# Four chains of four heads, or one chain of sixteen with its operands in DRAM: the RWKV-7 stage of a hybrid trunk

## The chip, the cores and the metric

The kernel runs on one core of a Trainium2 chip. The metric is the device time of one execution in microseconds. Five engines work beside each other: PE (TensorE, matrix products), DVE (VectorE), ACT (ScalarE), POOL (GpSimd) and SP (SyncE, which here issues nearly all DMAs). Each takes its instructions strictly in its own order and waits at an instruction until what it needs is there.

## The reference

One layer of a decoder trunk on x of 1 x 1024 x 1024, all float32: a normalised input goes through one projection to 7424 columns and from there into three branches (causal pooling, RWKV-7 time mixing, cross attention into 256 memory tokens), which are gated, merged and projected; a ConvFFN follows. The change touches the RWKV-7 branch: 16 heads of 64 values, each with a 64 x 64 state that runs through 1024 steps.

```python
def rwkv7_scan(r, w, k, v, kk_neg, kk_a):
    ...
    def step(state, inp):
        rt, wt, kt, vt, an, bn = inp
        sa = jnp.einsum('bhvk,bhk->bhv', state, an)
        state = state * wt[:, :, None, :] + sa[..., None] * bn[:, :, None, :] + vt[..., None] * kt[:, :, None, :]
        yt = jnp.einsum('bhvk,bhk->bhv', state, rt)
        return state, yt
...
    y = rwkv7_scan(rh, wh, kh, vh, -kk, kk * ah)
    mu = jnp.mean(y, axis=-1, keepdims=True)
    var = jnp.mean(jnp.square(y - mu), axis=-1, keepdims=True)
    y = ((y - mu) * lax.rsqrt(var + LNX_EPS)).reshape(B, S, RWKV_WIDTH)
    y = y * ln_x_w.astype(f32) + ln_x_b.astype(f32)
    bonus = jnp.sum(rh * kh * r_k.astype(f32), axis=-1, keepdims=True) * vh
    y = y + bonus.reshape(B, S, RWKV_WIDTH)
    return y.astype(dt) * g
```

## The kernel before

Everything lies with channels on the partitions and time along the row. The big projections keep float32 precision by splitting both operands into a high and a low part: mm3 (L165 to L171) issues three matmuls of 128x128 by 128x512, hh with whi, hl with whi and hh with wlo. These are the **wide** matmuls. in_block (L304) is one column block of the input projection: eight k by two halves of the time, 16 calls of mm3, 48 wides. Its weights come as four tiles wraw of 128 KB through SP, and ACT (L126) and POOL (L132) make whi and wlo of them.

The time of 1024 is cut into 16 chunks of 64 (C, NCH). Inside a chunk the recurrence is turned into products and a triangular system; from chunk to chunk a state is carried. The sixteen heads are eight pairs (two heads fill 128 partitions). rwkv_group (L455) handles two pairs, and it runs four times, g = 0 to 3. One group does, in this order:

- **Preparation**: decay and learning rate from two small products (psu), square sums of k for its norm (square_sums, L441, products phd), a scan and two exponentials, the r blocks by in_block, and on DVE and ACT the tiles AR, BK, then products ps1 and ps2 (L572, L579) of which masked parts go to NT, RB and AR, bonus (L530, to DRAM as d_bv), the scaling of BK, and its transposes pt to BKN (L595). HV holds the values, turned by the products pv.
- **Solve**: a triangular inverse of 32x32 blocks on DVE alone, a chain of 31 steps of two instructions each (L615, L617), with transposes at both ends (L609, L618, L619). Meanwhile fill_to(95 * g + 95) gives PE wide blocks to do that belong to the pool, query and gate columns and are needed by nothing here (L620; filled is the log, 16 entries to a block, so six blocks to a group). Then the result is copied into NT (L623), and products pz and pw (L631, L639) join the blocks.
- **Chain** (L653 to L716): 16 chunks, in each three **visits** of PE to small products of 64x64: pr (what the state gives the right-hand side), then py and pu (the system applied), then ph and py (the state and the output). After pr, DVE copies it to Rs; after pu, DVE and ACT copy its halves to HV; after ph, DVE adds the decayed state Hd; ACT makes the next Hd and copies py into AR.
- **Output norm** (L722 to L738): per pair, a square, a product pvar that sums it over a head, the root, three DVE steps with d_bv and d_g read from DRAM (gt), and d_y written.
- **group_kv** (L432): the k and v blocks of the next group, four in_blocks, evacuated by ACT and DVE (shifted, L309).

A scheduler lays the instructions of each engine out from a model of their durations; the code's order, the waits and hints by later (L206, an order without a semaphore) bind it. Where PE would wait, the scheduler puts in wides from blocks that stand later in the code. A chain chunk of one group has 20 small products; the wides between its visits come from the fill blocks and from group_kv. PSUM is eight banks: psg for wides (two tags by two), pss two, psk and psc one each. After the four groups the memory attention begins (products pmm, L787), with the eight fill blocks that are left.

Of the kernel before, what the change touches and what calls it, by code (L numbers as in the profile page):

```python
# [17 lines left out]
P = 128  # L18
T = 1024
# [25 lines left out]
def trunk_kernel(ctx: ExitStack, tc: tile.TileContext, xT, memT, pvec, w_in, w_kv, w_upd, w_upg,  # L45
# [19 lines left out]
    d_bv = dtile([8, P, T], "d_bv")  # L65
    d_y = dtile([8, P, T], "d_y")
# [237 lines left out]
    def in_block(j, evac, c=0, log=None):  # L304
        ws = load_w(w_in[j], KC, c=c)
        for t0, _ in HALVES:
            evac(t0, gemm(ws, hrhs(t0), log=log))
# [34 lines left out]
    ld = lr.tile([P, T], FR, name="ld")  # L342
    la = lr.tile([P, T], FR, name="la")
# [97 lines left out]
    def square_sums(src, scale, sq):  # L441

        sp = rw.tile([P, 2, 2, 512], FR, name="sp", tag="NT")
        for n, (t0, _) in enumerate(HALVES):
            s = slice(t0, t0 + 512)
            for d in (sp[:, n, 0], sq[:, s]):
                later(A.activation(d, src[:, s], AF.Square, scale=scale), late[0])
            V.tensor_tensor(sp[:, n, 1], sq[:, s], sp[:, n, 0].bitcast(F32), op=ALU.subtract)
        for n, (t0, _) in enumerate(HALVES):
            ps = pss.tile([P, 512], F32, name="phd", tag="s")  # L450
            PE.matmul(ps, bonesr, sp[:, n, 0], start=True, stop=False)
            PE.matmul(ps, bonesr, sp[:, n, 1], start=False, stop=True)
            yield slice(t0, t0 + 512), ps

    def rwkv_group(g, kv):  # L455
        tagA, tagB, tagC = ([f"X{i}{(g + n) % 3}" for i in range(2)] for n in range(3))
        AR = rw.tile([P, 2, 3, T], F32, name="AR", tag="AR")
        Dc = rw.tile([P, 2, NCH], F32, name="Dc", tag="Dc")
# [20 lines left out]
        table(LN_EXP)  # L479
        vs = []  # L480
# [9 lines left out]
        for i in range(2):  # L490
# [7 lines left out]
            for s, ps in square_sums(t0_, col("k_k", p), t5_):  # L498
                rstd(t5_[:, s], ps, 1)
# [7 lines left out]
            V.tensor_copy(Dc[:, i], c3(t3_)[:, :, C - 1])  # L507
# [37 lines left out]
        HV = rw.tile([P, 2, NCH, 2, C], F32, name="HV", tag="HV")  # L545
        for i in range(2):
            for c0 in (0, 8):
# [5 lines left out]
                A.copy(HV[64:128, i, c0:c0 + 8, 0], ps[64:128])  # L553
                A.copy(HV[0:64, i, c0:c0 + 8, 1], ps[0:64])

# [6 lines left out]
        for i in range(2):  # L562
            us = slice(NCH * i, NCH * i + NCH)
            for c0 in range(0, NCH, 4):
# [17 lines left out]
                V.tensor_tensor(c3(AR[lo, i, 2])[:, cs], ps[lo, :, 1], bc(mstrict, lo), op=ALU.mult)  # L582
            for b in range(2 if i == 0 else 0):
# [3 lines left out]
            for c in range(n):  # L587
                A.activation(BK[i][:, c], BK[i][:, c], AF.Identity, scale=Dc[:, i, c:c + 1])
            if n < NCH:
                V.tensor_tensor(BK[i][:, n:], BK[i][:, n:],  # L590
                                Dc[:, i, n:].unsqueeze(2).broadcast_to([P, NCH - n, P]), op=ALU.mult)
            for c0 in range(0, NCH, 4):
# [3 lines left out]
                A.copy(BKN[i][:, c0:c0 + 4], ps)  # L596

# [11 lines left out]
        V.transpose(X, S.rearrange("p u t -> p t u"))  # L609
# [10 lines left out]
        fill_to(95 * g + 95)  # L620
# [23 lines left out]
        for i in range(2):  # L644
            for e in range(2):
                V.tensor_tensor(RB[i][:, e], RB[i][:, e], mincl.unsqueeze(1).broadcast_to([P, NCH, C]),
                                op=ALU.mult)


        lo, up = slice(0, 64), slice(64, 128)  # L650
        Hn = rw.tile([P, 2, C], F32, name="Hn", tag="Hn")
        Hd = rw.tile([P, 2, C], F32, name="Hd", tag="Hd")
        turn = [0]  # L653

        def bank(name):
            turn[0] ^= 1
            return (psc if turn[0] else psk).tile([P, 2, C], F32, name=name, tag="c" if turn[0] else "k")

        def visit(products, after):

            for (out_, l, r), kw in products:
                m = PE.matmul(out_, l, r, **kw)  # L662
                if after is not None:
# [4 lines left out]
        ready = None  # L668
        for c in range(NCH):
            t = slice(c * C, (c + 1) * C)  # L670
            once = dict(start=True, stop=True)
            pr = bank("pr")
            py = pss.tile([P, 2, C], F32, name="py", tag="s")
# [6 lines left out]
            Rs = rw.tile([P, 2, C], F32, name="Rs", tag="Rs", bufs=1)  # L680
# [3 lines left out]
            for i in range(2 if c else 0):  # L684
                kw = dict(start=i == 0, stop=False)
                row.append(((py[lo, i], HV[lo, i, c, 0], AR[lo, i, 1, t]), kw))
                row.append(((py[up, i], HV[up, i, c, 1], AR[up, i, 1, t]), kw))
            row += [((pu[q, i], NT[q, i, c], Rs[q, i]), once) for i in range(2) for q in (lo, up)]
            visit(row, made if c else None)
            V.tensor_copy(HV[lo, :, c, 0], pu[lo])  # L690
            ready = A.copy(HV[up, :, c, 1], pu[up]).ins
            row = []
            if c + 1 < NCH:
                ph = bank("ph")
                for i in range(2):
                    row.append(((ph[up, i], BKN[i][:, c, 64:128], HV[:, i, c, 1]), once))
                    row.append(((ph[lo, i], BKN[i][:, c, 0:64], HV[:, i, c, 0]), once))
            for i in range(2):
                kw = dict(start=c == 0 and i == 0, stop=i == 1)
                row.append(((py[lo, i], HV[:, i, c, 0], RB[i][:, 0, c]), kw))  # L700
                row.append(((py[up, i], HV[:, i, c, 1], RB[i][:, 1, c]), kw))
            visit(row, ready)
            if c + 1 < NCH:
                for q, e in ((lo, 0), (up, 1)):
                    if c == 0:
                        ready = V.tensor_copy(HV[q, :, 1, e], ph[q]).ins
                    else:
                        ready = V.tensor_tensor(HV[q, :, c + 1, e], ph[q], Hd[q], op=ALU.add).ins  # L708
                if c + 2 < NCH:
# [4 lines left out]
                    for i in range(2):  # L714
# [5 lines left out]
        for i in range(2):  # L720
            p = 2 * g + i
            y = AR[:, i, 1]  # L722
            gt = rw.tile([P, 2, T], F32, name="gt", tag=tagA[i])
            SP.dma_start(gt[:, 0], d_bv[p])
            SP.dma_start(gt[:, 1], d_g[p])
            yq = rw.tile([P, T], F32, name="yq", tag=tagC[i])
            for t0, _ in HALVES:
                s = slice(t0, t0 + 512)
                sq = yq[:, s]
                A.activation(sq, y[:, s], AF.Square)  # L730
                ps = pss.tile([P, 512], F32, name="pvar", tag="s")
                PE.matmul(ps, bones, sq, start=True, stop=True)
                rstd(sq, ps, 2, 1.0 / 64)
                V.tensor_tensor(y[:, s], y[:, s], sq, op=ALU.mult)
# [974 lines left out]
```

## Time and profile before

| | us |
|---|---|
| runs | 2018.13, 2022.89, 2023.48 |
| median | 2022.89 |
| profiled execution | 2021.79 |
| its span | 2020.1 |
| RWKV stage, from the first psu to pmm | 95.2 to 972.0 |

The profile is one execution. Its page gives busy times by engine and by slices of the span; the timeline gives each instruction's start and length; the view of lines groups instructions by line, tile and shape with the mean of one; the view of waits says for which instruction of which engine an engine stood still. A tile on the left of an arrow is written, those on the right are read. One small product of the program shows up as two passes in the trace (x8 is four products), since a float32 product runs in two; a wide matmul is one. Lines of the profile are those of the code printed above.

### The profile page before, as it was taken

The page shows a single profiled execution, that of the slowest core. Times are in us where ns is not written, and L with a number is a line of the kernel's source. Part 1 is how long each engine was busy: PE and PEld are TensorE (multiplying, and loading weights), DVE is VectorE, ACT ScalarE, POOL GpSimd, SP SyncE. Part 2 cuts the span into 40 slices and gives each one's busy share as a digit, 9 for nine tenths or more (in the row PEclk, how much of TensorE's full clock was granted, in tenths as well). Part 3 has the DMA queues.
Part 4 walks back from the last instruction along what each step waited for, and adds up shares of the span by engine and source line. Part 5 has one row for each costly group of instructions (what it writes and reads, how often), then busy time and mean ns, then how long its engine had stood idle before and what let it go on. Part 6 is the DMA issues. An engine that isn't in the chain of part 4 may idle for free.

```text
span 2020.1 us, 34003 instructions
## 1 busy us (share of the span) xinstructions
PE 1977.1 (98%) x12218; PEld 1556.0 (77%) x12218; DVE 1374.0 (68%) x2227; ACT 1065.6 (53%) x2254; POOL 779.6 (39%) x867
## 2 busy tenths in 40 slices
PE   8999999999999999999999999999999999999997
PEld 6777767776778667776878888887878888888886
DVE  8577437664668347743696553658889888878698
ACT  6684348623773358434566334546554454545544
POOL 4411113121222122110232355555579988832441
PEclk9999999999999999999999999999999999999999
DMA  4312111120222121222525544545332222279776
GB/s 155 128 34 84 62 64 58 66 84 23 89 64 84 33 92 40 83 68 80 196 97 168 175 136 126 182 146 177 99 97 87 89 79 84 92 219 236 163 186 147
DMA packets 175689, 220.77 MB, mean 109 GB/s; under 512 B 16544, under 2 KB 127264, under 8 KB 175520
## 3 DMA queue, kind: packets, MB, share of 16 engines
q1 hardware_dynamic: 162592, 203.39, 31.1%
q0 software_dynamic: 11856, 14.16, 4.4%
q8 instruction: 96, 1.57, 0.3%
q10 hardware_dynamic: 1072, 1.05, 0.2%
q14 instruction: 73, 0.60, 0.1%
HBM read 169.25 MB, written 49.28 MB: 108 GB/s over the span
## 4 chain that ended last, share of the span: by engine, by line
PE 47%; DVE 2%; DMA 2%; issue 1%; ACT 0%; SPq 0%; POOL 0%; ACTq 0%; DVEq 0%; POOLq 0%
PE psg L168 7%; PE psg L170 7%; PE psg L169 7%; PE psf L169 5%; PE psf L170 5%; PE psf L168 5%; PE psd L169 3%; PE psd L170 3%; PE psd L168 3%; DMA Q<-in_w_fdn 1%; PE ptr L900 0%; DVE ts L842 0%; PE psn L1175 0%; PE po L168 0%; PE psco L170 0%
## 5 line engine op out<-in xcount | busy, mean ns | idle before, releaser
L132 POOL TENSOR_TENSOR wlo<-wraw,whi 128x256 fp32r<-128x256 f32 x464 | 393.8, 859 | 953.7 <-ACT whi L126 775.0
L168 PE MATMUL psg<-hh,whi 128*128 128x512 f32 x928 | 379.7, 409 | 11.4 <-ACT whi L126 5.9
L170 PE MATMUL psg<-hh,wlo 128*128 128x512 f32 x928 | 377.8, 407 | 0.4
L169 PE MATMUL psg<-hl,whi 128*128 128x512 f32 x928 | 377.4, 407 | 0.5 <-DVE hl L254 0.5
L126 ACT CAST whi<-wraw 128x256 fp32r<-128x256 f32 x472 | 182.2, 403 | 223.3 <-PE psg L169 109.1
L168 PEld LDWEIGHTS psg<-hh,whi 128*128 128x128 f32 x928 | 175.6, 189 | 51.2 <-ACT whi L126 5.9
L170 PEld LDWEIGHTS psg<-hh,wlo 128*128 128x128 f32 x928 | 175.4, 189 | 42.7 <-POOL wlo L132 5.8
L169 PEld LDWEIGHTS psg<-hl,whi 128*128 128x128 f32 x928 | 175.5, 189 | 39.8 <-issue 1.9
L1035 POOL TENSOR_TENSOR wt<-a,wt 128x256 fp32r<-128x256 f32 x136 | 156.6, 1175 | 35.9 <-ACT wt L1034 35.8
L169 PE MATMUL psd<-f,u 128*128 128x512 f32 x292 | 113.9, 390 | 0.2 <-DVE f L1451 0.2
L170 PE MATMUL psd<-f,u 128*128 128x512 f32 x292 | 113.8, 390 | 0.0
L168 PE MATMUL psd<-f,u 128*128 128x512 f32 x292 | 113.3, 391 | 0.2 <-ACT f L1447 0.2
L170 PE MATMUL psf<-h2h,wt 128*128 128x512 f32 x272 | 106.1, 390 | 0.9 <-POOL wt L1035 0.9
L168 PE MATMUL psf<-h2h,wt 128*128 128x512 f32 x272 | 106.0, 390 | 0.0
L169 PE MATMUL psf<-h2l,wt 128*128 128x512 f32 x272 | 106.0, 390 | 0.0
L1049 DVE SCALAR_TENSOR_TENSOR d<-z,pv,d 128x1023 f32<-128x1023 f32 x68 | 100.4, 1479 | 2.3
L708 DVE TENSOR_TENSOR HV<-ph,Hd 64x128 f32<-64x128 f32 x112 | 32.3, 289 | 72.7 <-PE ph L662 45.5
L1035 POOL TENSOR_TENSOR wt<-s,wt 128x256 fp32r<-128x256 f32 x68 | 79.6, 1189 | 3.5 <-ACT wt L1034 2.8
L169 PE MATMUL psf<-t,wt 128*128 128x512 f32 x204 | 79.5, 390 | 0.0
L170 PE MATMUL psf<-t,wt 128*128 128x512 f32 x204 | 79.5, 390 | 0.0
L168 PE MATMUL psf<-t,wt 128*128 128x512 f32 x204 | 79.5, 390 | 0.0
L1047 ACT ACTIVATE d<-z,pv 128x1024 f32<-128x1024 f32 x34 | 42.4, 1246 | 66.4 <-DVE z L1129 50.7
(429 smaller groups left out, 4708.2 us busy)
## 6 DMA issues: line engine op xcount, KB each, us to landing
wraw<-in_w_in SPq DMA_DIRECT2D x232, 128.0 KB, 2.4
a<-in_w_fup SPq DMA_DIRECT2D x128, 128.0 KB, 2.4
d_zg<-st SPq DMA_DIRECT2D x48, 256.0 KB, 2.7
wraw<-in_w_fup SPq DMA_DIRECT2D x80, 128.0 KB, 2.5
fraw<-d_f SPq DMA_DIRECT2D x33, 256.0 KB, 4.5
wraw<-in_w_prwkv SPq DMA_DIRECT2D x64, 128.0 KB, 2.5
wraw<-in_w_o SPq DMA_DIRECT2D x64, 128.0 KB, 2.6
d_f<-d SPq DMA_DIRECT2D x16, 512.0 KB, 3.4
```

What stands on the lines that cost most here:

```text
L126: i = A.copy(hi, src)
L132: (V if lo_on_dve[0] else G).tensor_tensor(lo, src, hi.bitcast(F32), op=ALU.subtract)
L168: first = PE.matmul(ps, wh, xh, start=start, stop=False)
L169: PE.matmul(ps, wh, xl, start=False, stop=False)
L170: last_mm[0] = PE.matmul(ps, wl, xh, start=False, stop=stop).ins
L708: ready = V.tensor_tensor(HV[q, :, c + 1, e], ph[q], Hd[q], op=ALU.add).ins
L1035: low = eng.tensor_tensor(w[1][:, us], src[u], w[0][:, us].bitcast(F32), op=ALU.subtract)
L1047: A.activation(d, z, AF.Identity, scale=col("cw2", j), bias=col("cb", j))
L1049: V.scalar_tensor_tensor(d[:, n:], z[:, :T - n], col(cw, j), d[:, n:], op0=ALU.mult, op1=ALU.add)
```

## The change

The four groups keep only the preparation and the solve. What the chain needs of them is written to DRAM (d_ar, d_rb, d_bk, d_nt, d_hv, laid out by pairs of chunks), and one function, chain, then runs the 16 chunks once for all eight pairs. A visit has four times the products, and each state tile (pr, pu, ph, Rs, Hn, Hd) is 128x512 instead of 128x128; copies out of PSUM are four times as wide and a quarter in number. The operands of two chunks come back by load(b), double-buffered.

The square sums of both pairs are made at the start of a group (lengths). The product of RB with mincl moves from after the solve to before the spill. group_kv of the next group moves from after the chain to before the solve, and the tags of the big tiles rotate by two instead of one. The fill blocks are dealt anew: up to entry 32, 48, 64 and 160 in the four solves (2, 1, 1 and 6 blocks), then inside the chain up to entry 172 + 148 * v // 47 ahead of visit v, and up to 384, all 24 blocks, after it. The output norm runs for two chunks at a time inside the chain (outputs), on all eight pairs. PSUM banks, the number of small products and the number of wides are the same.

```diff
+    d_ar = dtile([NCH // 2, P, 4, 2, 3, 2 * C], "d_ar")
+    d_rb = dtile([NCH // 2, P, 4, 2, 2, 2 * C], "d_rb")
+    d_bk = dtile([NCH // 2, P, 4, 2, 2, P], "d_bk")
+    d_nt = dtile([NCH // 2, P, 4, 2, 2 * C], "d_nt")
+    d_hv = dtile([NCH // 2, P, 4, 2, 2 * C], "d_hv")
...
     def group_kv(g, kv):
...
-            t = rw.tile([P, 2, T], F32, name=f"kv{i}", tag=f"X{i}{g % 3}")
+            t = rw.tile([P, 2, T], F32, name=f"kv{i}", tag=f"X{i}{2 * g % 3}")
...
     def rwkv_group(g, kv):
...
+        def lengths():
+            for i in range(2):
+                for s, ps in square_sums(kv[i][:, 0], col("k_k", 2 * g + i), tHV[:, i, 1], sp[:, i]):
+                    rstd(tHV[:, i, 1, s], ps, 1)
+
         if g:
+            lengths()
             table(SIGMOID)
...
+            for e in range(2):
+                V.tensor_tensor(RB[i][:, e], RB[i][:, e], mincl.unsqueeze(1).broadcast_to([P, NCH, C]),
+                                op=ALU.mult)
+                spill(d_rb, (g, i, e), RB[i][:, e])
+            for e in range(3):
+                SP.dma_start(d_ar[:, :, g, i, e].rearrange("c p t -> p c t"),
+                             AR[:, i, e].rearrange("p (c t) -> p c t", t=2 * C))
...
+        nxt = group_kv(g + 1, []) if g < 3 else None
         tb1 = rw.tile([P, 2, 32, 32], F32, name="tb1", tag=tagB[1])
...
-        fill_to(95 * g + 95)
+        if g == 3:
+            fill_to(96)
+        fill_to((32, 48, 64, 160)[g], solve if g == 3 else None)
...
+    def outputs(b, y, q):
+        bt = slice(b * 2 * C, (b + 1) * 2 * C)
+        gt = []
+        for src, e in ((d_bv, "ld"), (d_g, "la")):
+            gt.append(lr.tile([P, 8, 2 * C], F32, name="gt", tag=e))
+            SP.dma_start(gt[-1], src[:, :, bt].rearrange("n p t -> p n t"))
...
+        for n in (0, 4):
+            ns = slice(n, n + 4)
+            y_, q_ = y[:, ns], q.rearrange("p (n t) -> p n t", t=2 * C)
+            A.activation(q_, y_, AF.Square)
+            ps = pss.tile([P, 512], F32, name="pvar", tag="s")
+            PE.matmul(ps, bones, q, start=True, stop=True)
+            rstd(q, ps, 2, 1.0 / 64)
+            V.tensor_tensor(y_, y_, q_, op=ALU.mult)
...
+    def chain(fills):
...
+        def load(b):
+            ar, nt = ring[:, b % 2], pair[:, b % 2, 0]
+            hv = rw.tile([P, 8, 2, 2, C], F32, name="hv", tag=f"X{b % 2}2")
+            rb = rw.tile([P, 8, 2, 2 * C], F32, name="rb", tag=f"X{b % 2}1")
+            bk = rw.tile([P, 8, 2, P], F32, name="bk", tag=f"X{b % 2}0")
+            for q, e in ((up, 0), (lo, 1)):
+                SP.dma_start(hv[q, :, :, e], d_hv[b, q].rearrange("p g i (u s) -> p (g i) u s", u=2))
+            SP.dma_start(ar, d_ar[b].rearrange("p g i e t -> p (g i) e t"))
+            SP.dma_start(nt, d_nt[b].rearrange("p g i t -> p (g i) t"))
+            SP.dma_start(bk, d_bk[b].rearrange("p g i u s -> p (g i) u s"))
+            SP.dma_start(rb, d_rb[b].rearrange("p g i e t -> p (g i) e t"))
...
         def visit(products, after):
-            for (out_, l, r), kw in products:
+            wide = fill_to(fills(visits[0]))
+            visits[0] += 1
+            for n, ((out_, l, r), kw) in enumerate(products):
                 m = PE.matmul(out_, l, r, **kw)
+                if n == 0:
+                    later(m, wide)
...
+        load(0)
+        load(1)
         for c in range(NCH):
+            b, u = divmod(c, 2)
+            if u == 0 and 0 < b < NCH // 2 - 1:
+                load(b + 1)
...
-            for i in range(2):
-                row.append(((pr[up, i], AR[ko, i, 2, t], HV[ko, i, c, 1]), once))
-                row.append(((pr[lo, i], AR[ke, i, 0, t], HV[ke, i, c, 0]), once))
+            for i in range(8):
+                row.append(((pr[up, i], ar[ko, i, 2, t], hv[ko, i, u, 1]), once))
+                row.append(((pr[lo, i], ar[ke, i, 0, t], hv[ke, i, u, 0]), once))
...
-            A.copy(AR[:, :, 1, t], py)
+            A.copy(y[:, :, t], py)
+            if u:
+                outputs(b, y, root)
...
     for g in range(4):
         kv = rwkv_group(g, kv)
+    chain(lambda v: 172 + 148 * v // 47)
+    fill_to(384)
```

How the instructions stand shows in the order of each engine. PE before, one chunk in the chain of a group (psg is a wide, the others small products; x4 is four in a row):

```order
L662 MATMUL pr<-HV,AR 64x64 x4
L170 MATMUL psg<-hh,wlo 128x512
L662 MATMUL py<-AR,HV 64x64 x4
L662 MATMUL pu<-Rs,NT 64x64 x4
L168 MATMUL psg<-hh,whi 128x512
L169 MATMUL psg<-hl,whi 128x512
L170 MATMUL psg<-hh,wlo 128x512
L168 MATMUL psg<-hh,whi 128x512
L662 MATMUL ph<-HV,BKN_7881 64x64 x2
L662 MATMUL ph<-HV,BKN_7882 64x64 x2
L662 MATMUL py<-RB_7879,HV 64x64 x2
L662 MATMUL py<-RB_7880,HV 64x64 x2
```

PE after, one chunk in the single chain (hv, ring, pair, bk and rb are the tiles loaded from DRAM, in the places of HV, AR, NT, BKN and RB):

```order
L738 MATMUL pr<-hv,ring 64x64 x16
L173 MATMUL psg<-hh,whi 128x512
L738 MATMUL py<-ring,hv 64x64 x16
L738 MATMUL pu<-Rs,pair 64x64 x16
L174 MATMUL psg<-hl,whi 128x512
L175 MATMUL psg<-hh,wlo 128x512
L173 MATMUL psg<-hh,whi 128x512
L174 MATMUL psg<-hl,whi 128x512
L175 MATMUL psg<-hh,wlo 128x512
L173 MATMUL psg<-hh,whi 128x512
L174 MATMUL psg<-hl,whi 128x512
L738 MATMUL ph<-hv,bk 64x64 x16
```

Each stretch of small products is four times as long, and there is one such chunk where there were four. In other chunks a gap between visits holds up to some forty wides.

DVE before, where the solve of the second group begins (tb are its tiles; from L615 the 31 steps follow, without a break):

```order
L590 TENSOR_TENSOR BK_3130<-BK_3130,Dc 128x1024
L604 COPY tb_3615<-NT 32x512 x2
L646 TENSOR_TENSOR RB_3492<-RB_3492,mincl 128x1024
L609 STREAM_TRANSPOSE tb_3615<-tb_3615 128x1024
L610 MEMSET tb_3615 128x1024
L611 MEMSET tb_3615 128x32
L615 TENSOR_TENSOR tb_3721<-tb_3615 128x31
L617 TENSOR_TENSOR tb_3615<-tb_3615,tb_3721 128x31
```

DVE after, the same place (kv are the k and v of the next group, sp its square sums):

```order
L598 TENSOR_TENSOR RB_2621<-RB_2621,mincl 128x1024
L611 TENSOR_TENSOR BK_2258<-BK_2258,Dc 128x1024
L627 COPY tb_2752<-NT 32x512 x2
L324 SCALAR_TENSOR_TENSOR kv_2866<-zc,pv,kv_2866 128x1
L326 SCALAR_TENSOR_TENSOR kv_2866<-psg,pv,kv_2866 128x511
L633 STREAM_TRANSPOSE tb_2752<-tb_2752 128x1024
L454 TENSOR_TENSOR sp<-tHV,sp 128x512
L634 MEMSET tb_2752 128x1024
L322 COPY zc<-psg 128x1
L326 SCALAR_TENSOR_TENSOR kv_2866<-psg,pv,kv_2866 128x511
L635 MEMSET tb_2752 128x32
```

The evacuations of the next group's k and v and the subtractions of its square sums now stand among the steps of the solve.

SP after, one block of two chunks in the chain (wraw are weights of the wides):

```order
L719 DMA ring<-d_ar 128x3072
L718 DMA hv<-d_hv 64x16x64 x2
L720 DMA pair<-d_nt 128x1024
L721 DMA bk<-d_bk 128x2048
L699 DMA d_y<-pair 128x8x128
L722 DMA rb<-d_rb 128x2048
L163 DMA wraw<-in_w_in 128x256 x2
L686 DMA gt<-d_bv 128x8x128
L686 DMA gt<-d_g 128x8x128
```

The loads of ring, hv, pair, bk and rb are new. Before, gt was read and d_y written after each chain, and in the chains only weights and spilled fill blocks passed through SP.

More of the change, by code (lines that the diff above doesn't have):

```diff
@@ new lines, in chain @@
+    def chain(fills):
+        lo, up = slice(0, 64), slice(64, 128)
+        ring = rw.tile([P, 2, 8, 3, 2 * C], F32, name="ring", tag="AR")
+        pair = rw.tile([P, 2, 2, 8, 2 * C], F32, name="pair", tag="HV")
+        state = rw.tile([P, 4, 8, C], F32, name="Rs", tag="NT")
+        Rs, Hn, Hd = (state[:, n] for n in range(3))
+        root = state[:, 3].rearrange("p n t -> p (n t)")
+        held = {}
+        def load(b):
[9 more added lines that the diff above has]
+            SP.dma_start(rb, d_rb[b].rearrange("p g i e t -> p (g i) e t"))
+            held[b] = ar, nt, hv, rb, bk, pair[:, b % 2, 1]
@@ L683, in rwkv_group @@
             row = []
-            for i in range(2 if c else 0):
+            for i in range(8 if c else 0):
                 kw = dict(start=i == 0, stop=False)
[L686 to L691, printed above, removed]
+                row.append(((py[lo, i], hv[lo, i, u, 0], ar[lo, i, 1, t]), kw))
+                row.append(((py[up, i], hv[up, i, u, 1], ar[up, i, 1, t]), kw))
+            row += [((pu[q, i], nt[q, i, t], Rs[q, i]), once) for i in range(8) for q in (lo, up)]
+            visit(row, made)
+            V.tensor_copy(hv[lo, :, u, 0], pu[lo])
+            ready = A.copy(hv[up, :, u, 1], pu[up]).ins
             row = []
```

118 lines of the change are left out of this document (54 added, 64 removed).

## The prediction, made before the change was run

> **What bounds the kernel now.** I read the page first: busy times, then the slices.
>
> ```profile
> span 2020.1 us, 34003 instructions
> PE 1977.1 (98%) x12218; PEld 1556.0 (77%) x12218; DVE 1374.0 (68%) x2227; ACT 1065.6 (53%) x2254; POOL 779.6 (39%) x867
> PE   8999999999999999999999999999999999999997
> ```
>
> PE is busy in every slice. The change touches the RWKV stage only, so I cut that out by windows (columns: window, its length, busy time and instructions of PE, PEld, DVE, ACT, POOL, the clock, the DMA share, GB/s); the second row is the first group's chain, the third and fourth are the heaviest DMA stretches elsewhere. The last row heads the list of PE's waits inside the stage (total, times, longest).
>
> ```profile
> 95.20:972.00 876.80, 864.10 (x7135) 639.20 (x7133) 520.64 (x1028) 471.69 (x1012) 174.18 (x209) 1.00 0.20 67
> 224.00:298.00 74.00, 74.00 (x975) 49.68 (x969) 26.76 (x88) 28.67 (x83) 7.77 (x12) 1.00 0.12 40
> 1080.00:1120.00 40.00, 39.79 (x196) 32.75 (x196) 20.94 (x35) 28.89 (x57) 9.39 (x11) 1.00 0.73 241
> 1820.00:1840.00 20.00, 20.00 (x90) 16.57 (x89) 19.45 (x31) 9.26 (x17) 6.44 (x5) 1.00 1.11 263
> PE pv L551 <- ACT HV L554: 2.9, 3, 1.1
> ```
>
> PE stands idle 12.7 us of 876.8 at full granted clock, and the largest of its waits is 2.9 us in all. So what counts is how long PE's own instructions take, and whether the change makes PE wait where it does not now. A busy PE need not be an efficient one: the timeline of PE (start, length, instruction) shows how its starts are spaced. First a run of nothing but wide matmuls in the solve of the second group, 65 from the first row to the last:
>
> ```profile
> 427.62 0.39 PE L169 MATMUL psg<-hl,whi 128*128 128x512 f32 x1
> ...
> 442.13 0.39 PE L170 MATMUL psg<-hh,wlo 128*128 128x512 f32 x1
> ```
>
> (442.13 − 427.62)/64 = **0.2267 us per wide**. Now one whole chunk of a chain, from one pr to the next, and the view of one tile in it (duration of one pass, min/median/max):
>
> ```profile
> 237.06 0.45 PE L662 MATMUL pr<-HV,AR 128*64 128x64 f32 x8
> 237.44 0.49 PE L170 MATMUL psg<-hh,wlo 128*128 128x512 f32 x1
> 237.87 0.45 PE L662 MATMUL py<-AR,HV 64*64 64x64 f32 x8
> 238.15 0.40 PE L662 MATMUL pu<-Rs,NT 64*64 64x64 f32 x8
> 238.48 0.50 PE L168 MATMUL psg<-hh,whi 128*128 128x512 f32 x1
> 238.81 0.39 PE L169 MATMUL psg<-hl,whi 128*128 128x512 f32 x1
> 239.04 0.40 PE L170 MATMUL psg<-hh,wlo 128*128 128x512 f32 x1
> 239.28 0.40 PE L168 MATMUL psg<-hh,whi 128*128 128x512 f32 x1
> 239.60 0.45 PE L662 MATMUL ph<-HV,BKN 128*64 128x64 f32 x8
> 239.89 0.40 PE L662 MATMUL py<-RB,HV 128*64 128x64 f32 x8
> 240.22 0.50 PE L169 MATMUL psg<-hl,whi 128*128 128x512 f32 x1
> 240.56 0.40 PE L170 MATMUL psg<-hh,wlo 128*128 128x512 f32 x1
> 240.88 0.45 PE L662 MATMUL pr<-HV,AR 128*64 128x64 f32 x8
> L662 PE MATMUL py<-AR,HV x8: 218/218/267, 237.9 to 238.1; 64*64 64x64 f32 x8
> ```
>
> The chunk takes 240.88 − 237.06 = 3.82 us. It holds 7 wides (1.59 us) and 20 small products, each of two passes. Eight passes cover 0.40 us (row 238.15) of which the last is 0.218, so their starts lie within 0.18 us, three steps from the first product to the fourth: 0.06 us per product, 1.20 for 20. What is left, 3.82 − 1.59 − 1.20 = 1.03 us, is spread over the three places where PE goes from wides to small products and back: **0.34 us per visit**. The rows show it: wide to wide is 0.2267, but pr starts 0.38 before the wide behind it though it has four products, and the wide after a visit (238.48) is 0.33 before the next.
>
> **The change part by part.** Products and wides stay the same in number; only their grouping changes.
>
> *Visits.* Counting, in the order of PE, the places between the first psu and pmm where wides give way to anything else, I get 331 before and 151 after (chains alone: 217 and 51). 180 × 0.34 = **−62 us**. The bounds: with the row gap of 0.28 us for four products (237.87 to 238.15) a product is at most 0.07, a visit at least (3.82 − 1.59 − 1.40)/3 = 0.28, which gives −50; I take −62 since that gap holds the start of the visit too.
>
> *Solve.* The triangular solve runs on DVE alone, and PE covers it with wides. Two rows of PE, one of DVE, and three groups of DVE (busy, mean ns, idle before):
>
> ```profile
> 389.28 1.14 PE L579 MATMUL ps<-AR,BK 64*128 64x128 f32 x8
> 430.62 4.36 DVE L623 COPY NT<-tb 32x512 f32<-32x512 f32 x8
> 442.45 0.73 PE L631 MATMUL pz<-tb,NT 32*32 32x32 f32 x34
> L321 DVE SCALAR_TENSOR_TENSOR kv<-psg,pv,kv 128x511 f32<-128x511 f32 x25 | 18.6, 743 | 0.0
> L448 DVE TENSOR_TENSOR sp<-tHV,sp 128x512 fp32r<-128x512 f32 x14 | 12.0, 876 | 0.0
> L646 DVE TENSOR_TENSOR RB<-RB,mincl 128x1024 f32<-128x1024 f32 x16 | 21.2, 1324 | 0.3
> ```
>
> In the second group DVE needs from the end of the last ps (390.4) to the end of the placing copies (435.0) 44.6 us, and pz starts at 442.45: 7.5 us to spare. PE's cover there is 221 wides (50.1 us) and 2.0 us of transposes. After the change the second and third groups have 167 wides and four psu: 37.9 + 2.0 + 0.9 = 41 us. And DVE gets more: seven evacuations of the next group's k and v (7 × 0.743 = 5.2 us), four subtractions of the square sums (3.5 us), less one RB product that now stands earlier (1.3 us): 52 us. So PE waits 11 us at pz in each of the two: **+22 us**. In the first group 226 wides (51.2 + 2.0) meet the same 52, in the last 192 (43.5 + 2.0) meet 43: nothing. Bounds: nothing, if DVE's extra work finds room in the spare 7.5 us of now and is placed behind the solve, and twice that, 44, if DVE also waits in its order for k and v blocks that PE has not made yet.
>
> *The chain's evacuations.* A state tile grows from 128x128 to 128x512. DVE and ACT rows of such shapes, and one of the small ones now:
>
> ```profile
> L537 DVE TENSOR_TENSOR kv<-kv,pbo 128x512 f32<-128x512 f32 x16 | 10.5, 680 | 0.1
> L553 ACT COPY HV<-pv 64x512 f32<-64x512 f32 x16 | 9.3, 580 | 6.1 <-DVE kv L526 5.8
> L681 DVE COPY Rs<-pr 128x128 f32<-128x128 f32 x64 | 18.6, 290 | 53.0 <-PE pr L662 53.0
> L691 ACT COPY HV<-pu 64x128 f32<-64x128 f32 x64 | 16.7, 260 | 63.7 <-DVE HV L690 63.6
> ```
>
> pr to pu: the copy takes 0.68 instead of 0.29, and between them lie a wide and 16 py products (0.23 + 0.96). pu to ph: DVE's copy and then ACT's (the last row shows that ACT waits for DVE), 0.68 + 0.58 = 1.26, against seven wides (1.59). ph to pr: two additions, at most 1.36, against 16 products and two wides (1.41). All three are covered, the last one barely. The Trainium skill, "TensorEngine Tiling (Array Packing)", section PSUM Bottleneck, warns that making TensorE faster does nothing for the copies out of PSUM, which can then become what limits; by that rule the saving would be partly taken back here, and the rows above say it would be by tenths of a microsecond per visit, the fourth rival below. One chunk has no wides at two of these places; I add 2 us for it.
>
> *Output norm in the chain.* Its 16 pvar products, two passes each, existed before.
>
> ```profile
> L732 PE MATMUL pvar<-yq,bonesr 128*128 128x512 f32 x32 | 15.6, 595 | 0.0
> L730 ACT ACTIVATE yq<-AR x16: 615/622/636, 297.6 to 953.9; 128x512 f32<-128x512 f32 x16
> ```
>
> Now the first of a block waits for a square on ACT (0.62) that starts only after the y copy (0.58 by the ACT row above), while PE has two wides and 13 products (1.23 us), and ACT's Hd work may stand in between. I take 1 us for each of eight blocks, **+8** (0 to 24).
>
> *DRAM.* The operands go out and come back. Out: 9.4 MB per group, about 75 GB/s more over a preparation of some 126 us (its instructions at the durations above) on the stage's 67, so I price it at nothing; SP's queue waits there for each product that it spills, and the weights behind it are then up to a DVE product (1.3 us) late, inside their lead. Back: per two chunks ring 1.57, bk and rb 1.05 each, hv and pair 0.52 each, 4.72 MB. The chain with its own weights, spills, gt and y moves 60.8 MB, of which 9.4 are loaded ahead: 51.4. The chain on PE is 480 wides (108.8), 1232 products (73.9), 16 pvar (15.6) and 50 visits (17): 215 us, so 239 GB/s. A chain now uses the DMA engines by 0.12. The rows above hold 241 GB/s for 40 us and 263 for 20 beside a PE that is 99 to 100% busy. So the loads fit, but weights behind a burst land later than now (2.4 us, below), and four weight tiles in flight are about 4 us of wides: **+5** (0 to 15). At the start, the last spill and the read behind it are one after the other (issues by kind, KB each, median us to landing):
>
> ```profile
> wraw<-in_w_in SPq DMA_DIRECT2D x184, 128.0 KB, 2.4
> d_bv<-kv SPq DMA_DIRECT2D x8, 512.0 KB, 3.0
> gt<-d_bv SPq DMA_DIRECT2D x8, 512.0 KB, 4.8
> ```
>
> With several such tiles queued I estimate 12 us against some 40 wides (9 us) between the last pw and the first pr: **+3**.
>
> Sum: −62 + 22 + 2 + 8 + 5 + 3 = −22. From the profiled execution's 2021.8 (span 2020.1 and 1.7 around it) this gives 2000; the median of the runs is 2022.9, 1.1 above it, within what runs differ by (2018.1 to 2023.5).
>
> **Rivals.** About 0.3%, 6 us, is what a measurement can tell from no change.
>
> (a) *The waits are hidden*: DVE's extra work and the output norm find room, only the visits count, 1960 to 1980. For it: DVE is busy 521 of 877 us. Against it: the solve is one unbroken DVE run.
>
> (b) *The DMA cannot hold the rate*, on the slower side. No row shows over 40 us at 241 GB/s, and none with so many scattered pieces: the loads fetch 512-byte rows, and hv is written in 256-byte pieces. The chain takes 51.4 MB over the rate, so below 51.4/(215 + 22) = 217 GB/s the change loses; at 200 GB/s the chain takes 257 us, 42 more, and the kernel 2000 + 42 − 5 = 2037 (the 5 us for late weights are in it then). The Trainium skill, "DMA: Bandwidth & Descriptors", section Specifications, asks for at least 512 bytes for full rate; no row here shows the price of smaller pieces, and by that rule (b) would be the case.
>
> (c) *DVE's solve costs more*: DVE stands in its order behind k and v evacuations that PE has not yet made, so PE waits up to twice as long, 44 instead of 22: 2022 at most, mostly 2010 to 2020. About no change.
>
> (d) *The PSUM copies limit the visits*: 48 visits × 0.3 us = 14 us more, 2014.
>
> **How the numbers follow.** Forecast (1983 to 2010) 0.46, (a) 0.17, (b) 0.15, (c) 0.14, (d) 0.08. Faster by over 0.3% (below 2017): forecast, (a), half of (d), a fifth of (c): 0.70. Within: 0.12. Slower: (b) and a few of (c): 0.18. The range leaves out the lower end of (a) and the upper of (b): 1966 to 2034.
>
> **What would show it.** Right: PE's visits with 16 and 32 products at 0.06 us each; PE waits of 10 to 15 us at pz in the second and third groups, released by DVE's placing copy, and hardly any in the others; PE waits of about 1 us at pvar released by ACT; a chain of 215 to 230 us at a DMA share near 0.8. Wrong: waits of PE for whi released by wraw all along the chain (b), pz waits of over 20 us (c), a wait in front of nearly every pu, ph and pr (d), or a visit that costs more the longer it is, which would shrink the first term.

## The result, and the profile after

| | before | after |
|---|---|---|
| median of 5 runs, us | 2023.48 (2018.13 to 2027.15) | 2035.83 (2032.70 to 2039.66) |
| profiled execution, span, us | 2020.1 | 2037.9 |
| RWKV stage, first psu to pmm, us | 876.8 (2301 wides) | 847.6 (2112 wides) |
| PE idle in the stage, us | 12.7 | 54.1 |
| TensorE at half clock in the stage, us | 0 | 81.9 |

The ratio after to before is 1.0063, with a 95% interval of 1.0039 to 1.0087: slower by 12 us, where I had forecast 2000 us. First the page of the changed kernel, the rows that answer to those of before:

```profile
span 2037.9 us, 33739 instructions
PE 1950.6 (96%) x12218; PEld 1574.1 (77%) x12218; DVE 1346.7 (66%) x2015; ACT 1048.9 (51%) x2158; POOL 779.2 (38%) x867
PE   7999998998988989899999999999999999999997
PEclk9999999979988999999999999999999999999999
```

PE issues as many instructions as before and is busy 26 us less, yet the span is 18 us longer. The fourth row says where to look: PEclk, the granted clock of TensorE, has dips in slices 9, 12 and 13, while the window of the whole stage showed 1.00 before. The windows view of the changed kernel, over the whole stage and over four stretches of it (columns as in the prediction):

```profile
96.50:944.10 847.60, 793.46 (x6946) 621.67 (x6945) 492.29 (x814) 441.35 (x891) 167.44 (x193) 0.95 0.52 154
420.00:440.00 20.00, 20.00 (x69) 15.12 (x69) 9.36 (x18) 8.69 (x24) 0.00 (x0) 0.50 0.48 131
580.00:600.00 20.00, 14.57 (x69) 12.38 (x69) 11.31 (x19) 12.45 (x28) 0.00 (x0) 0.59 0.84 242
645.00:665.00 20.00, 13.91 (x209) 10.69 (x210) 1.39 (x2) 4.48 (x10) 2.82 (x4) 0.58 0.66 212
672.40:909.00 236.60, 218.44 (x2999) 171.01 (x2999) 94.65 (x135) 103.65 (x249) 30.19 (x39) 0.97 0.75 216
```

From 420 to 440 us PE is busy all the time, at a clock of 0.50, and gets 69 instructions done. The last row is the chain, from the first pr to the last pvar: 236.6 us, in which PE is idle for 18.2 us. The waits of PE in the stage (total, times, longest):

```profile
PE psg L173 <- ACT whi L131: 19.2, 3, 7.5
PE psu L488 <- DVE tb L639: 9.2, 2, 4.9
PE ps L593 <- DVE AR L589: 5.4, 4, 2.6
PE ps L586 <- DVE AR L596: 2.6, 7, 1.2
```

And PE's timeline at the four longest of them (the bracket gives the idle time ahead and who ended it):

```profile
355.12 0.76 PE L488 MATMUL psu<-la,uhi 128*128 128x512 f32 x1 [4.91 <-DVE tb L639]
...
412.76 1.54 PE L593 MATMUL ps<-AR,BK 64*128 64x128 f32 x6 [2.64 <-DVE AR L589]
...
651.33 0.80 PE L173 MATMUL psg<-hh,whi 128*128 128x512 f32 x1 [6.00 <-ACT whi L131]
651.92 0.63 PE L174 MATMUL psg<-hl,whi 128*128 128x512 f32 x1
...
740.25 0.80 PE L173 MATMUL psg<-hh,whi 128*128 128x512 f32 x1 [7.49 <-ACT whi L131]
740.84 0.63 PE L174 MATMUL psg<-hl,whi 128*128 128x512 f32 x1
```

Behind them the instructions take longer: after the waits for whi a wide that lasted 0.39 us in a run of wides lasts 0.63 to 0.80, and the next one starts 0.59 us later instead of 0.23. One compact chunk of the chain, undisturbed, shows the gain of the change:

```profile
712.82 1.15 PE L738 MATMUL ph<-hv,bk 128*64 128x64 f32 x32
713.80 1.10 PE L738 MATMUL py<-rb,hv 128*64 128x64 f32 x32
714.84 0.50 PE L174 MATMUL psg<-hl,whi 128*128 128x512 f32 x1
715.17 0.40 PE L175 MATMUL psg<-hh,wlo 128*128 128x512 f32 x1
715.58 1.15 PE L738 MATMUL pr<-hv,ring 128*64 128x64 f32 x32
716.66 0.49 PE L173 MATMUL psg<-hh,whi 128*128 128x512 f32 x1
717.08 1.15 PE L738 MATMUL py<-ring,hv 64*64 64x64 f32 x32
718.07 1.10 PE L738 MATMUL pu<-Rs,pair 64*64 64x64 f32 x32
719.10 0.50 PE L174 MATMUL psg<-hl,whi 128*128 128x512 f32 x1
...
720.58 0.40 PE L174 MATMUL psg<-hl,whi 128*128 128x512 f32 x1
720.91 1.15 PE L738 MATMUL ph<-hv,bk 128*64 128x64 f32 x32
```

From one ph to the next, 8.09 us hold 80 products (4.80 at 0.06), ten wides (2.27) and three visits: (8.09 − 4.80 − 2.27)/3 = 0.34 us per visit, as before, with four times the products in it.

### The profile page after: what moved, and what is told of

Same layout as the page of the kernel before. It is cut to its first block, busy times and chain, and to the rows that moved or that the text cites. A ratio compares the mean times of both kernels' runs of the same rounds, so it can differ in the third digit from the quotient of the medians.

```text
span 2037.9 us, 33739 instructions
## 1 busy us (share of the span) xinstructions
PE 1950.6 (96%) x12218; PEld 1574.1 (77%) x12218; DVE 1346.7 (66%) x2015; ACT 1048.9 (51%) x2158; POOL 779.2 (38%) x867
## 4 chain that ended last, share of the span: by engine, by line
PE 49%; DVE 1%; DMA 1%; issue 0%; ACT 0%; POOL 0%; SPq 0%; ACTq 0%; DVEq 0%; POOLq 0%
PE psg L175 7%; PE psg L173 7%; PE psg L174 7%; PE psf L175 5%; PE psf L173 5%; PE psf L174 5%; PE psd L174 3%; PE psd L175 3%; PE psd L173 3%; PE ptr L964 0%; DMA d_f<-ug 0%; PE psn L1239 0%; PE po L173 0%; DMA wraw<-in_w_fup 0%; DMA kvr<-in_w_kv 0%
## 5 line engine op out<-in xcount | busy, mean ns | idle before, releaser
L137 POOL TENSOR_TENSOR wlo<-wraw,whi 128x256 fp32r<-128x256 f32 x464 | 398.1, 870 | 961.6 <-ACT whi L131 912.4
L175 PE MATMUL psg<-hh,wlo 128*128 128x512 f32 x928 | 372.7, 402 | 2.6 <-POOL wlo L137 2.4
L1098 ACT CAST wt<-a 128x256 fp32r<-128x256 f32 x136 | 50.7, 404 | 42.2 <-POOL wt L1099 23.4
```

Of the source, the lines that this page charges most:

```text
L137: (V if lo_on_dve[0] else G).tensor_tensor(lo, src, hi.bitcast(F32), op=ALU.subtract)
L175: last_mm[0] = PE.matmul(ps, wl, xh, start=False, stop=stop).ins
L1098: A.copy(w[0][:, us], src[u])
```

## The experiments

The theory after the result: the visits save what was forecast, and it is lost in PE's waits **and in a half clock behind them**. The rivals: the DMA engines cannot hold the chain's rate (the forecast's rival b), and DVE stays the bound of the solves. Twelve runs follow, one of them the changed kernel again. Each ratio is to the kernel before on the same chip (medians 2023.9 to 2024.3). The edits are against the changed kernel and shown in part; ... marks what is left out.

**The same kernel twice.** No edit.

> The changed kernel once more, for a second profile. Theory (half clock): PE's waits are the same to 1 us, but the stretches at half clock differ (82 us in the first profile's RWKV stage), and the stage is longer or shorter by about half their difference. Rival (the clock costs nothing that the waits don't): the stage's length follows the waits alone.

2029.7 us, span 2028.0. PE's idle time in the stage is 54.4 us (54.1 in the first profile), with the same wait of 2.64 us in front of the ps of the third group. The windows of this second execution:

```profile
95.60:929.80 834.20, 779.77 (x6945) 611.18 (x6944) 492.60 (x814) 439.86 (x890) 168.88 (x193) 0.97 0.53 157
417.00:437.00 20.00, 19.83 (x110) 14.49 (x110) 14.23 (x28) 12.91 (x34) 0.74 (x1) 1.00 0.64 193
```

The place that ran at 0.50 for 27.3 us in the first profile (the record of the granted clock has it from 412.8 to 440.1) ran at half clock for 3.4 us here, and the stage is 13.4 us shorter with the same waits. The busy time at half clock is 37.0 us against 68.7; half of the difference is 15.9, somewhat more than the stage lost. So the clock costs time of its own, and it differs between executions of one program.

That gives an account to hold against every run: the stage's length, less PE's idle time, less half of its busy time at half clock. If nothing else matters, the rest is the same for all kernels with the same work. (Idle time is what lies between PE's instructions, and the half clock is taken from the record behind the PEclk row.)

| kernel | stage | idle | busy at half clock | rest |
|---|---|---|---|---|
| before | 876.8 | 12.7 | 0 | 864.1 |
| changed, first profile | 847.6 | 54.1 | 68.7 | 759.1 |
| changed, second profile | 834.2 | 54.4 | 37.0 | 761.3 |
| e1_store | 829.7 | 47.5 | 43.7 | 760.3 |
| e2_deal | 819.2 | 39.3 | 36.4 | 761.7 |
| e3_noload | 820.1 | 38.6 | 42.7 | 760.2 |
| e4_both | 809.0 | 31.9 | 28.5 | 762.9 |
| e5_spread | 838.0 | 56.1 | 41.6 | 761.2 |
| e6_noout (16 pvar fewer) | 809.0 | 41.4 | 48.4 | 743.4 |
| e7_three | 816.1 | 42.6 | 18.3 | 764.4 |
| e9_rb | 826.8 | 46.6 | 37.9 | 761.2 |
| e10_three | 807.3 | 32.7 | 23.0 | 763.1 |
| e11_actq | 859.1 | 70.0 | 60.1 | 759.0 |
| e12_four | 821.5 | 45.3 | 25.3 | 763.6 |

The rest is 759 to 764 us for all that do the same work, over stages that differ by 52 us. It is not quite constant: it falls as the half clock grows, from 764.4 at 18.3 us to 759.0 at 60.1, so one half is too high a price. A straight line through the twelve profiles with the same work gives 0.39 of the busy time at half clock, and a rest of 766 without any. The 189 wides that move behind the stage are 42.8 us; 864.1 − 42.8 = 821.3, so the grouping of visits is worth 821.3 − 761 = **60 us**, or 56 by the straight line.

**The solves.** Two fill blocks move from behind the chain into the solves of the second and third group.

```diff
         if g == 3:
-            fill_to(96)
-        fill_to((32, 48, 64, 160)[g], solve if g == 3 else None)
+            fill_to(96 + 32)
+        fill_to((32, 64, 96, 192)[g], solve if g == 3 else None)
...
-    chain(lambda v: 172 + 148 * v // 47)
+    chain(lambda v: 204 + 148 * v // 47)
```

> The changed kernel with two fill blocks taken from behind the chain: one more in the solve of the second group and one more in that of the third (entries 32, 64, 96, 192; the chain starts at 204, 32 entries stay behind it). Theory (DVE's solve): the waits at psu of 4.9 us (at 350) and 4.3 us (at 497) and the smaller ones beside them (1.4 us) go, with 2 x 3.4 us of half clock (3.4 us worth): 2036 - 10.6 - 3.4 = about 2022. Rival (DVE stays the bound, PE then waits at pz instead): 2032 to 2040.

2008.7 us (ratio 0.9925, 0.9909 to 0.9941): faster than both kernels, and 27 us under the changed one, where 14 were expected. Both waits at psu are gone and none took their place at pz. In the solve of the third group PE waits for DVE once more, at pw, and that short wait is followed by 10 us at half clock, in which PE runs mostly 32x32 products (behind the same wait of 0.98 us in e4 and e12 there is none). The timeline, and the window behind it:

```profile
501.88 0.40 PE L175 MATMUL psg<-hh,wlo 128*128 128x512 f32 x1
503.26 0.92 PE L665 MATMUL pw<-NT,tb 32*32 32x32 f32 x46 [0.98 <-DVE tb L661]
```

```profile
504.50:514.60 10.10, 10.10 (x134) 7.72 (x128) 0.70 (x1) 4.18 (x7) 0.00 (x0) 0.50 0.24 66
```

Part of the gain is not the solve's: the wait at the chain's start fell from 6.0 to 0.96 us as well; SP's order came out differently there.

**The chain's start.** SP's queue there, in the changed kernel (start, time in the queue's issue):

```profile
629.42 0.33 SPq L163 DMA_DIRECT2D wraw<-in_w_in  x1
636.46 0.33 SPq L722 DMA_DIRECT2D rb<-d_rb  x1
...
639.06 1.44 SPq L163 DMA_DIRECT2D wraw<-in_w_in  x3
```

Nothing leaves SP for 7 us; the waits of SP name the rb load, whose tile the solve still uses, and the weights stand behind it:

```profile
SPq L722 <- DVE NT L649: 6.7, 1, 6.7
```

The experiment binds the first two rb loads behind the last spill of the solve (solved lists the spills of d_nt).

```diff
...
-            SP.dma_start(rb, d_rb[b].rearrange("p g i e t -> p (g i) e t"))
+            i = SP.dma_start(rb, d_rb[b].rearrange("p g i e t -> p (g i) e t"))
+            if b < 2:
+                later(i, solved[-1].ins)
```

> The changed kernel with one thing moved: the rb loads of the first two blocks are bound behind the last spill of the solve, since rb lies in the solve's tiles. Theory (SP's queue in order): the 6.0 us wait for whi at the chain's start comes from SP standing 7 us at the rb load until the solve has left its tiles, with the weights behind it; it goes with 10 to 17 us of half clock (5 to 7 us): 2034 - 6 - 6 = about 2022. Rival (the DMA engines are full there): the wait stays, 2029 to 2040.

2018.0 us (ratio 0.9977, 0.9963 to 0.9991), 18 us under the changed kernel with this edit alone. The wait of 6.0 us is gone, and there is no half clock between 590 and 713 us. The chain's waits for whi stay (11.4 us in all, longest 6.8).

**The waits inside the chain.** Here SP stands at the store d_y, which waits for the output norm, and at loads that wait for PE to leave a buffer (waits of SP between 600 and 910 us, then its queue ahead of PE's wait of 7.49 us):

```profile
SPq L699 <- DVE pair L698: 40.5, 7, 7.9
SPq L718 <- PE py L738: 17.1, 5, 4.4
```

```profile
726.82 0.43 SPq L722 DMA_DIRECT2D rb<-d_rb  x1
735.07 0.37 SPq L699 DMA_DIRECT2D d_y<-pair  x1
735.56 2.40 SPq L163 DMA_DIRECT2D wraw<-in_w_in  x3
```

PE has stood still since 732.8 when the weights leave at 735.56. The store one chunk later:

```diff
-        SP.dma_start(d_y[:, :, bt].rearrange("n p t -> p n t"), y)
+        return lambda: SP.dma_start(d_y[:, :, bt].rearrange("n p t -> p n t"), y)
...
+            if owed:
+                later(owed.pop()(), ready)
             if u:
-                outputs(b, y, root)
+                owed.append(outputs(b, y, root))
+        owed.pop()()
```

> The changed kernel with one thing moved: the store d_y of a pair of chunks stands one chunk later in the code, bound behind the next chunk's state. Theory (SP's queue): the waits for whi of 7.5 us (at 733) and 5.7 us (at 831) come from SP standing 7.9 us at the d_y store, with the weights queued behind it; moved, both waits go, and the two stretches of 6.8 us at half clock behind them too (about half of the 7 us that are not idle, 3.5 us): 2036 - 13 - 3.5 = about 2019. Rival (DMA rate): the weights are late because the DMA engines are full; the waits stay, 2032 to 2040.

2025.5 us (1.0011, 1.0000 to 1.0022): 10 us gained of the 17 expected. The waits fell from 7.5 and 5.7 us to 4.7 and 1.8; SP's time at the store fell from 40.5 to 14.0 us. The rest of the waits is not the store's. Next, no loads behind the first two blocks:

```diff
             if u == 0 and 0 < b < NCH // 2 - 1:
-                load(b + 1)
+                held[b + 1] = held[b - 1]
```

> The changed kernel without the loads of the third to eighth pair of chunks: the chain works on the operands of the first two again (leaves out 28 MB of reading; its output is not the reference's). Theory (SP's queue): the waits at 733 and 831 stay, since the d_y store still stands ahead of the weights; only small waits go: 2030 to 2040. Rival (DMA rate): the chain's waits for whi behind its start go, 13 us and 3.5 us of half clock: 2016 to 2022.

2004.4 us: both waits vanish, though the store stands where it stood. So my expectation was wrong, and it looked like the rival's. But without loads SP's order also changes, so rate and order are not told apart by it. The next kernel tries that: the same loads at about the same time from ACT's queue.

```diff
+            q_ = SP if b < 2 else A
...
-            SP.dma_start(ar, d_ar[b].rearrange("p g i e t -> p (g i) e t"))
+            q_.dma_start(ar, d_ar[b].rearrange("p g i e t -> p (g i) e t"))
```

> The changed kernel with the chain's operand loads of the third to eighth block issued from ACT's queue in place of SP's; the same bytes, asked for at about the same time. Theory (SP's queue in order): the waits for whi of 7.5 and 5.5 us in the chain fall below 2 us each, with 3.5 us of half clock: 2034 - 10 - 3.5 = about 2020. Rival (DMA rate): the weights land as late behind the same bytes, 2029 to 2040.

2049.0 us (1.0111, 1.0093 to 1.0129): slower, but the waits bear on the question. PE in the stage:

```profile
PE pvar L693 <- ACT Rs L691: 16.8, 6, 3.1
PE ph L739 <- ACT hv L775: 13.3, 6, 3.1
...
PE psg L173 <- ACT whi L131: 6.6, 1, 6.6
```

The only wait for whi left is the one at the chain's start. In place of the others PE waits 30 us in all for the square and the pu copy, both on ACT. That is not shown to be the loads' doing: the edit also changed the order of PE, and in five of the eight blocks no wide stands between the two pvar, where the changed kernel has 13 to 15. The chain became 258 us long, so the same 51 MB moved at 198 GB/s instead of 216. This run alone therefore does not part order from rate; e5 below moves its bytes faster.

Order is also not the whole of it. The view of DMAs says how long weights took that had left SP (KB each, median us to landing): those of the chain's start, from 639 us, then those behind the two long waits at d_y, from 735 and from 830.

```profile
wraw<-in_w_in SPq DMA_DIRECT2D x3, 128.0 KB, 11.6
wraw<-in_w_in SPq DMA_DIRECT2D x3, 128.0 KB, 3.9
wraw<-in_w_in SPq DMA_DIRECT2D x3, 128.0 KB, 5.8
```

Before, the median was 2.4 us. SP's standing sends the weights late, and right behind the operand loads it had held back they also land late; at the chain's start that second part is the larger. e9, which takes the standing away, takes the other part with it: there the weights landed in 2.3 to 5.7 us.

**Loads in pieces, and no output norm.** e5 loads only the first block ahead and asks for the next tiles one by one, each bound behind a step of the chain.

```diff
-        load(1)
...
+        jobs = []
+
+        def piece(ins):
+            if jobs:
+                later(jobs.pop(0)(), ins)
...
             made = V.tensor_copy(Rs, pr).ins
+            piece(made)
...
             ready = A.copy(hv[up, :, u, 1], pu[up]).ins
+            piece(ready)
...
-            A.copy(y[:, :, t], py)
+            piece(A.copy(y[:, :, t], py).ins)
```

> The changed kernel with its loads spread: the operands of the next two chunks are asked for one tile at a time, each bound behind a step of the chain, and only the first block is loaded ahead of the chain. Nothing else moves. Theory (bursts of loads ahead of the weights): the waits for whi of 6.0, 7.5 and 5.7 us go or fall below 2 us each, with most of the half clock behind them (31 us in the profile of the change, of which about 20 not idle, 10 us): 2036 - 15 - 8 = about 2013. Rival (the d_y store and the output norm alone block the queue): only the first wait changes, about 2028.

2030.1 us (1.0026, 1.0012 to 1.0041). The waits at 733 and 831 went; two of 2.5 and 0.9 us for whi are left in the chain. Its chain moved 55 MB at 228 GB/s, faster than the changed kernel's 216, and its weights landed after 4.0 us in the median against 3.2. So a higher rate and slower landings came with shorter waits for weights, which the rival of rate can't explain. But pvar (7.6 us) and ph (6.1 us) now wait, with no wide between the two pvar of two blocks, and the chain's start waits 6.65 us as before, since SP still stands 8.0 us at the rb load ahead of the weights. Neither the theory's 2013 nor its mechanism held in full. e6 leaves the output norm out.

```diff
             if u:
-                outputs(b, y, root)
+                SP.dma_start(d_y[:, :, b * 2 * C:(b + 1) * 2 * C].rearrange("n p t -> p n t"), y)
```

> The changed kernel with the output norm left out of the chain (y is stored as it is: no square, pvar, root, product with d_g; its output is not the reference's). Theory (loads and norm together fill SP's queue and the DMA engines): 16 pvar (15.6 us) go, gt is not loaded, d_y waits for ACT's copy alone, so the waits at 733 and 831 go with 3.5 us of half clock, and the 6.0 us at the chain's start stays: 2036 - 16 - 13 - 3.5 = about 2003. Rival (loads alone): the waits stay, 2036 - 16 = 2020.

1994.7 us, below the expected 2003: one wait of 1.8 us for whi is left in the chain, and the rest of the account is 743.4, 18 us less, about the 16 pvar (15.6 us).

**Together.** e4 is e1 with e2.

> e1 and e2 together. Theory: 2036 - 16.5 - 14 = about 2005, faster than both kernels. Rival (DMA rate, DVE bound): 2030 to 2040.

2005.1 us (0.9912, 0.9880 to 0.9943), as expected. With the loads of e5 besides:

> Fill blocks dealt as in e2, the store as in e1 and the loads as in e5. Theory: of e4's waits (4.7, 1.5, 1.7 us for whi) most go, with 10 to 20 us of half clock: 2005 - 7 - 7 = about 1991. Rival (the waits are the DMA engines' mean rate, not its bursts): as e4, 2000 to 2008.

2010.3 us (0.9932, 0.9914 to 0.9951): not better, the waits of e5 at pvar and ph came along. With the rb of e9 in place of e5's loads:

> e4 (blocks dealt anew, store moved) and e9's rb together. Theory: e4's wait of 1.7 us at the chain's start and the 10 us of half clock behind it go: 2005 - 2 - 4 = about 1999. Rival: as e4, 2001 to 2009.

**1999.6 us** (0.9876, 0.9849 to 0.9904), the fastest of those that do the whole work, 25 us under the kernel before on its chip. And with the loads on ACT:

> e10 and e11 together. Theory: 1999 - 6 - 2 = about 1991. Rival: as e4, 2001 to 2009.

2020.6 us (0.9989, 0.9967 to 1.0011): e11's waits for ACT at pvar and ph came along.

## Why the prediction was wrong, point by point

The account of the two profiles, 2037.9 − 2020.1 = +17.8 us: visits −62 (821.3 − 759.1), idle time +41, half clock +34 (half of 68.7), behind the stage +3, ahead of it +1. In the second profile the half clock is +18.5 and the span 10 us shorter. By the straight line above the visits are −56 and the half clock is +27 and +14.

- **The step that failed** is the sum itself: "Sum: −62 + 22 + 2 + 8 + 5 + 3 = −22". It prices every wait at its own length. In the first profile seven waits of 2.0 to 7.5 us each have a stretch in or behind them in which PE works at half speed, 3.4 to 27.3 us long. That term, 14 to 34 us, was missing: without it the two profiles would lie 7 to 17 us below the kernel before, not 8 and 18 above. The trace of before had the evidence, outside the stage: one of its few waits over 2 us, at 1386 us, and the windows on and behind it.

```profile
1386.44 1.60 PE L1175 MATMUL psn<-s,ones 128*128 128x512 f32 x2 [2.61 <-DVE s L1170]
```

```profile
1387.00:1390.40 3.40, 3.40 (x9) 2.31 (x8) 2.15 (x5) 3.25 (x5) 1.21 (x2) 0.50 0.52 119
1390.40:1393.80 3.40, 3.40 (x16) 2.81 (x15) 3.40 (x7) 3.23 (x8) 0.68 (x1) 1.00 0.23 81
```

  In a slice of the page, 50 us, a stretch of 3.4 us does not show. The Trainium skill, "TensorE: Matmul & The Clock Gate", Part 1, says that TensorE falls to half rate after an idle window of about 3.4 us and comes back after one busy window. The shortest stretches here, 3.4 us, agree; that waits of 2.6 us and less are enough, and that a busy PE stayed at half for 27.3 us, differ, and here the runs decide.

- **Visits**: right in kind and nearly in size, −62 in one profile and −60 in the other (−56 by the line), and 0.34 us per visit with 16 and 32 products in it.
- **Idle time as a whole**: forecast +40, measured +41, but by compensating errors. The *solve* was put at 22 us at pz; it was 9.2 at psu, whose PSUM bank DVE frees only between its steps (its copy of the bank ended at 354.97, psu started at 355.12), so PE met the same DVE bound one place earlier. *Late weights* were put at 5 and *the chain's start* at 3; together they were 19.2 us. The burst of bytes that I had priced was real, with landings of 3.9 to 11.6 us, but the larger part in the chain was another mechanism: SP standing at one DMA for 7 to 8 us with the weights behind it. I had counted the loads' bytes and not what each load waits for. The *preparation*, priced at nothing, has 12.0 us of waits at ps and pt for DVE and ACT, against 1.3 before; that this is for want of wides there was not tried. The *output norm* was put at 8 and was 1.5, the chunk without wides 2 and was 2.8.
- **Rival (b)**, the slower side: its time came out by coincidence. The chain took 237 us at a DMA share of 0.75 and 216 GB/s, longer than the 215 to 230 forecast and just below the 217 GB/s named as the point of loss. But without PE's 18.2 us idle and 3 us for the half clock it is the 215 us of the forecast, and e5 moved its bytes at 228 GB/s with shorter waits for weights. The reading of the pieces was wrong as well: the operand loads came in rows of 4096 to 12288 bytes, not 512, and hv alone in pieces of 256, each of which took 32 ns in the chain where one of 512 took 30.
- **Rival (d)**: PE waited 2.8 us for PSUM copies at ph and pr in the whole chain. The rule on evacuation of the Trainium skill, "TensorEngine Tiling (Array Packing)", section PSUM Bottleneck, did not bite here.
- **Rival (c)** and the range: DVE's share was smaller than forecast. The range ended at 2034; only rival (b) reached further, and no term of mine made a wait cost more than its length.

## What to carry to other kernels

An idle PE can cost more than the idle time: when a change trades many short switches for a few waits, expect a stretch of half speed behind most waits of about 2 us or more (in the stage of the thirteen profiles, 59 of the 62 waits of 2.6 us or more had one in them or within 3.4 us behind, and 13 of the 21 from 2.0 to 2.6), and look up in the profile of before what its longest waits were followed by. On a queue that issues in order, a load is as dangerous by what it waits for as by its bytes: ask for each new DMA what stands behind it, and bind it behind the moment when its buffer is free, not merely ahead of its use. Wides that cover a wait may be worth most where small products follow: the two blocks moved into the solves gained 27 us, though part of that came from the chain's start.

## What the runs showed of the hardware

- Half clock comes in pieces of 3.41 us: the stretches in the profiles last 3.4, 6.8, 10.2, 13.7, 17.1, 20.5 and 27.3 us. In eight profiles the program is the same up to the wait of 2.6 us at about 410 us; it was followed by 27.3 us of half clock in one, by 6.8 in one and by 3.4 in six. The long stretches all lie over small products (ps, pt, pv, pz, pw) with few wides; where wides follow, as after the waits in the chain, they end after 3.4 to 10.2 us.
- The changes of the clock in a profile all lie on one grid of 3.41 us, and what counts is how long PE is idle within one step of it, not the wait as such. In the thirteen profiles of changed kernels (60 to 1000 us), a step at full clock with 2.0 us or more of idle time was followed by half clock in 75 of 75 cases; with 1.5 to 2.0 us in 14 of 36, with 1.0 to 1.5 in 4 of 83, with less in 3 of 1980, these three over small products. So a wait of 2 to 3 us can escape when the grid cuts it in two, as one of 2.18 us did in e7, and the same program can fare differently from one execution to the next.
- Of the steps at half clock with PE busy for at least 2.8 us, none of 29 with seven or more wides was followed by another, and 27 of 47 without a wide were. That PE's load has to be dense for the clock to return fits this, but it was not tried by itself.
- The stage differed by 13 us between two profiles of one program with the same waits. The spread of the changed kernel's runs (7 us) is of that order.
